# Adding the squares of the latents on VectorE ahead of each latent norm's product with ones

## The chip, the cores and the metric

The kernel runs on one core of a Trainium2 chip. The metric is the device time of one execution in microseconds (us). Before the change the median of three runs is 800.81 us (800.29 to 801.99).

## What is computed

One layer of a decoder trunk on 512 tokens of width 1024: an input projection feeds three branches (a causal pooling mixer, multi-head latent attention, cross-attention into 256 memory tokens), which are gated, merged, projected and added to the residual; then a two-level mixture of experts (32 experts, two per token) and a last RMSNorm. The change touches only the two latent norms of the attention branch, which in the reference are

```
def rms_norm(x, g):
    xf = x.astype(jnp.float32)
    xf = xf * lax.rsqrt(jnp.mean(xf * xf, axis=-1, keepdims=True) + RMS_EPS)
    return xf.astype(x.dtype) * g
...
    c_q = rms_norm(q_down, q_norm_g)
...
    c_kv = rms_norm(kv_down, kv_norm_g)
```

`q_down` has 384 and `kv_down` 256 channels per token, both cut from the input projection of the normalised tokens.

## The kernel before

**Layout.** In the first stage activations stand transposed: a tile has 128 channels on the partitions and the 512 tokens along the free axis. The kv latent is thus two tiles (`zk`), the q latent three (`zq`). The sum of squares over channels is a sum over partitions and tiles. It is made on TensorE (PE) by a product with a 128x128 matrix of ones, which also spreads it to all partitions: one product per tile, accumulated in one PSUM bank.

**Units.** `inproj(c)` (line 278) makes one 128x512 output tile of the input projection. Weights and activations are split into a high and a low fp32r part, so a unit is 24 matmuls of 128x128 by 128x512: 16 on lines 198 and 199 (high weights) and 8 on line 201 (low weights). The weights of unit c+2 are split when unit c is written down: the cast to the high part on ScalarE (ACT, line 180), the subtraction for the low part on GpSimd (POOL, line 125).

**Order of the work.** The whole program stands under a manual schedule: every engine runs its instructions in the order in which the Python code writes them down, and an instruction that waits holds up all that is behind it on its engine. Each unit's result goes to one of four PSUM banks (`mmb`). VectorE (DVE) takes it out by `scaled` (line 283, times the token norm `rx`), then ACT squares it (line 288). Between these stand the preparations of the memory tokens, `mem_prep` (lines 308 to 319): on ACT two scaled copies (line 132) and a square (line 315), on DVE two scalar_tensor_tensor (line 133) and an addition of squares (line 319). `latent_norm` writes the products with ones (line 294), the square root on ACT (line 136) and the reciprocal on DVE (line 137); `latent_end` scales the latent (line 300) and splits it. The places around the two latent norms:

```
    p4 = inproj(4)
    mem_prep(1)
    zq.append(scaled(p3, gt))
    sq_.append(squared(zq[1]))
    rk = latent_norm(sk)
    p5 = inproj(5)
    zq.append(scaled(p4, gt))
    sq_.append(squared(zq[2]))
    for i in range(2):
        latent_end(zk[i], rk, P_KV + i, ckv)
...
        pu = inproj(6 + gi)
        if gi == 0:
            kr = scaled(p5, gt)
            rq = latent_norm(sq_)
            mem_prep(2)
```

So the order on PE is p4, the norm of the kv latent (two products), p5, the first pooling unit pu0, the norm of the q latent (three products), and the other pooling units. DVE lags behind PE: at the kv norm it still has `mem_prep(1)` and the taking out of p3 ahead of it.

**Later stages.** Gates, cross-attention, latent attention and the output projection run up to some 500 us; then come 16 pairs of experts, whose weights (line 686) go by 512 KB pieces into a ring of 40 places, each loaded once its place is free.

Of the kernel before, what the change touches and what calls it, by code (L numbers as in the profile page):

```python
# [14 lines left out]
OP = mybir.AluOpType  # L15
# [26 lines left out]
def trunk_and_moe(ctx, tc, a, out):  # L42
    nc = tc.nc
    v, s, g, pe = nc.vector, nc.scalar, nc.gpsimd, nc.tensor
# [54 lines left out]
    def gt(dt=F32, shape=(128, 512)):  # L99
        return G1.tile(list(shape), dt, tag="g", name=nm("g"), bufs=36)  # L100

    def mt(dt=F32, shape=(128, 512)):
        return G2.tile(list(shape), dt, tag="m", name=nm("m"), bufs=6)
# [7 lines left out]
    def mmb():  # L111
        return bank(PA, "mm", 4)
# [5 lines left out]
    ones = K[:, C_ONES:C_ONES + 128]  # L118
# [16 lines left out]
    def rsqrt(dst, ms, inv):  # L135
        s.activation(dst, ms, AF.Sqrt, bias=eps[:, 0:1], scale=inv)
        v.reciprocal(dst, dst)
# [152 lines left out]

    def latent_norm(sq):
        ps = mmb()
        for i, q in enumerate(sq):
            pe.matmul(ps, lhsT=ones, rhs=q, start=i == 0, stop=i == len(sq) - 1)
        r = gt()
        rsqrt(r, ps, 1.0 / (128 * len(sq)))
        return r
# [41 lines left out]
    ps = mmb()  # L339
# [21 lines left out]
# [5 lines that stand above are left out]
# [11 lines left out]
    for gi, w in enumerate(WINDOWS):  # L377
# [5 lines that stand above are left out]
# [114 lines left out]
    for h_ in range(XHEADS):  # L497
# [3 lines left out]
        ps = mmb()  # L501
# [31 lines left out]
    for h_ in range(XHEADS):  # L533
# [22 lines left out]
        ps = mmb()  # L556
# [78 lines left out]
    for d in range(KD):  # L635
        w = WS.use("w_bpm", d)
        res = []
        for j, y in enumerate((yp, ym)):
            ps = mmb()
# [160 lines left out]
    for h_ in range(HEADS):  # L800
        for op in SEQ:
            k, i = op[0], op[1:]
# [138 lines left out]
    for d in range(KD):  # L941
# [14 lines left out]
        sq = mt()  # L956
# [522 lines left out]
```

## Time and profile before

| | |
|---|---|
| median of 3 runs | 800.81 us (800.29 to 801.99) |
| the profiled execution | 801.2 us, of which the span of the trace is 799.4 us |
| PE busy | 775.8 us, 97% of the span |
| DVE busy | 366.3 us, 46% |
| ACT busy | 303.6 us, 38% |
| POOL busy | 277.1 us, 35% |
| mean granted TensorE clock | 0.992 |

Busy time of an engine says only that it had work in flight. The matmuls are pipelined, so a single matmul's duration is longer than its distance to the next one, and the cost of one is read from the distance of starts. Times in the rows count from the start of the span. "PEld" is the loading of the stationary operand, "PEclk" the granted clock as a share of full speed.

### The profile page before, as it was taken

How to read it: one execution, taken by the hardware profiler on the slowest of the kernel's cores; microseconds unless marked ns; L12 is line 12 of the kernel's file. 1: busy time of each engine (PE TensorE's matmuls, PEld its weight loads, DVE VectorE, ACT ScalarE, POOL GpSimd, SP SyncE). 2: the span in 40 equal slices, each digit the busy share in tenths (PEclk: the TensorE clock that was granted, in tenths of full speed). 3: DMA queues.
4: the chain of work that ended last, by engine and by line, in shares of the span. 5: the costliest groups of instructions: out<-in, count | busy, mean ns of one | idle time of the engine just before them, and what ended most of it. 6: DMA issues, size and time to landing. Idle time of an engine off the chain costs nothing. (4 is left out here: it accounts for less than half of the span.)

```text
span 799.4 us, 10154 instructions
## 1 busy us (share of the span) xinstructions
PE 775.8 (97%) x3743; PEld 523.8 (66%) x3743; DVE 366.3 (46%) x673; ACT 303.6 (38%) x623; POOL 277.1 (35%) x169
## 2 busy tenths in 40 slices
PE   7999999999999999999999999999999999999995
PEld 3778888888887888788888888854333333333432
DVE  5669684243446134677774433142212122454544
ACT  6254354343345544655653321122232223122223
POOL 3156676543241689522222924230212122000000
PEclk8999999999999999999999999999999999999998
DMA  6532333322221322211115379988999999999963
GB/s 220 186 106 106 106 106 132 132 80 80 80 79 43 110 89 82 64 47 57 54 54 211 132 277 342 374 289 307 392 378 383 402 367 388 408 372 390 409 264 121
DMA packets 53509, 164.17 MB, mean 205 GB/s; under 512 B 7906, under 2 KB 9058, under 8 KB 53456
## 3 DMA queue, kind: packets, MB, share of 16 engines
q1 hardware_dynamic: 46224, 149.14, 50.8%
q0 software_dynamic: 4640, 9.90, 3.9%
q10 hardware_dynamic: 2592, 4.46, 1.5%
q8 instruction: 30, 0.49, 0.3%
q14 instruction: 23, 0.19, 0.1%
HBM read 158.82 MB, written 11.53 MB: 213 GB/s over the span
## 5 line engine op out<-in xcount | busy, mean ns | idle before, releaser
L125 POOL TENSOR_TENSOR wl<-r,wh 128x1024 fp32r<-128x1024 f32 (+3 forms) x75 | 167.9, 2245 | 211.2 <-ACT wh L180 191.3
L180 ACT CAST wh<-r 128x1024 fp32r<-128x1024 f32 (+3 forms) x85 | 82.1, 972 | 31.8 <-PE mm L199 12.6
L1131 PE MATMUL gu<-e,u 128*64 128x512 f32 x336 | 88.5, 607 | 1.4 <-DMA e<-in_w_e 1.4
L198 PE MATMUL mm<-g,wh 128*128 128x512 f32 x180 | 71.9, 400 | 0.0
L199 PE MATMUL mm<-g,wh 128*128 128x512 f32 x180 | 70.2, 390 | 0.0
L1107 ACT ACTIVATE u<-xe,PR 128x128 f32<-128x128 f32 x120 | 34.3, 368 | 67.1 <-PE xe L1103 67.0
L471 PE MATMUL mm<-box,wh 128*128 128x512 f32 x144 | 56.8, 394 | 0.9 <-ACT wh L180 0.9
L472 PE MATMUL mm<-box,wh 128*128 128x512 f32 x144 | 56.2, 391 | 0.0
L201 PE MATMUL mm<-g,wl 128*128 128x512 f32 x180 | 52.6, 391 | 0.0
L1161 POOL DMA_INDIRECT xo<-y,ix x9 | 14.3, 1594 | 89.8 <-DVE ix L1082 79.7
L435 ACT ACTIVATE m<-s,st 128x256 f32<-128x256 f32 (+3 forms) x48 | 24.4, 509 | 54.5 <-DVE st L433 54.0
L1131 PEld LDWEIGHTS gu<-e,u 128*64 128x64 f32 x336 | 20.5, 135 | 33.7 <-issue 26.3
L1170 PE MATMUL y<-e,u 128*64 128x512 f32 x160 | 38.6, 600 | 0.6 <-DMA e<-in_w_e 0.6
L201 PEld LDWEIGHTS mm<-g,wl 128*128 128x128 f32 x180 | 33.8, 188 | 7.4 <-POOL wl L125 0.2
L198 PEld LDWEIGHTS mm<-g,wh 128*128 128x128 f32 x180 | 34.0, 189 | 6.4
L199 PEld LDWEIGHTS mm<-g,wh 128*128 128x128 f32 x180 | 33.9, 188 | 6.4
L476 PE MATMUL mm<-box,wl 128*128 128x512 f32 x144 | 36.6, 390 | 0.0
L198 PE MATMUL mm<-box,wh 128*128 128x512 f32 x78 | 31.7, 406 | 0.9 <-DVE g L283 0.9
L1157 DVE TENSOR_SCALAR y<-y,it 128x512 f32<-128x512 f32 x9 | 6.8, 751 | 54.1 <-PE y L1170 54.1
L471 PEld LDWEIGHTS mm<-box,wh 128*128 128x128 f32 x144 | 27.1, 188 | 6.7 <-ACT wh L180 1.3
L476 PEld LDWEIGHTS mm<-box,wl 128*128 128x128 f32 x144 | 27.0, 188 | 5.8
L472 PEld LDWEIGHTS mm<-box,wh 128*128 128x128 f32 x144 | 27.1, 188 | 5.3
(358 smaller groups left out, 1650.2 us busy)
## 6 DMA issues: line engine op xcount, KB each, us to landing
e<-in_w_e SPq DMA_DIRECT2D x124, 512.0 KB
r<-in_w_in SPq DMA_DIRECT2D x37, 512.0 KB
r<-in_w_e SPq DMA_DIRECT2D x15, 512.0 KB
wh<-in_w_e SPq DMA_DIRECT2D x15, 512.0 KB
wl<-in_w_e SPq DMA_DIRECT2D x15, 512.0 KB
m<-in_w_e SPq DMA_DIRECT2D x30, 256.0 KB
r<-in_w_bpm SPq DMA_DIRECT2D x8, 512.0 KB
r<-in_w_bl SPq DMA_DIRECT2D x8, 512.0 KB
```

What stands on the lines that cost most here:

```text
L125: eng.tensor_tensor(lo, x, hi.bitcast(F32), op=OP.subtract)
L180: s.copy(hi[:, :cols], r[:, :cols])
L198: pe.matmul(ps, lhsT=lh, rhs=rh, start=start and i == 0, stop=False)
L199: pe.matmul(ps, lhsT=lh, rhs=rl, start=False, stop=False)
L201: pe.matmul(ps, lhsT=ll, rhs=rh, start=False, stop=stop and i == m - 1)
L435: s.activation(P[:, :w], S[:, :w], AF.Exp, bias=st4[:, 0:1], accum_out=st4[:, 1:2])
L471: pe.matmul(ps, lhsT=lh, rhs=rh, start=k == 0, stop=False)
L472: pe.matmul(ps, lhsT=lh, rhs=rl, start=False, stop=False)
L476: pe.matmul(ps, lhsT=ll, rhs=rh, start=False, stop=k == KD - 1)
L1107: s.activation(x[:, j], ps[:, j], AF.Copy, scale=PR[:, k:k + 1])
L1131: pe.matmul(gu[r], lhsT=self.xe[k // 4][:, k % 4, r], rhs=self.wts[b][k], start=k == 0, stop=k == KD - 1)
L1170: pe.matmul(y[r], lhsT=self.aT[:, k, r], rhs=self.wts[b][8 + 2 * k + hf], start=k == 0 and not more, stop=k == 1)
```

## The change

`latent_norm` adds the squares into the first one on DVE and issues one product with ones. For the kv norm this is one addition and one product where there were two products; for the q norm two additions and one product where there were three.

```
@@ -290,8 +290,9 @@
     def latent_norm(sq):
         ps = mmb()
-        for i, q in enumerate(sq):
-            pe.matmul(ps, lhsT=ones, rhs=q, start=i == 0, stop=i == len(sq) - 1)
+        for q in sq[1:]:
+            v.tensor_tensor(sq[0], sq[0], q, op=OP.add)
+        pe.matmul(ps, lhsT=ones, rhs=sq[0], start=True, stop=True)
         r = gt()
         rsqrt(r, ps, 1.0 / (128 * len(sq)))
         return r
```

The lines below it move down by one: line 294 is now the addition, line 295 the product.

**PE at the kv norm.** In the names, mm_386 is p4, mm_424 the norm's bank, mm_436 p5; g_333 and g_335 are the squares of the kv latent, K holds the ones. Before:

```order
L201 MATMUL mm_386<-u_134,wl_299 128x512
L294 MATMUL mm_424<-g_333,K 128x512 [waits DVE_49,Activation_49]
L294 MATMUL mm_424<-g_335,K 128x512 [waits Activation_49]
L198 MATMUL mm_436<-box_126,wh_337 128x512 [waits DVE_49,Activation_49]
L199 MATMUL mm_436<-box_126,wh_337 128x512
```

and now:

```order
L201 MATMUL mm_386<-u_134,wl_299 128x512
L295 MATMUL mm_424<-g_333,K 128x512 [waits DVE_49]
L198 MATMUL mm_436<-box_126,wh_337 128x512 [waits Activation_49]
L199 MATMUL mm_436<-box_126,wh_337 128x512
L198 MATMUL mm_436<-box_127,wh_337 128x512
```

One product is gone, and the one that stays now reads what DVE wrote last in this place; its wait for ACT's square has become a wait for DVE's addition.

**DVE at the two norms.** g_374 and g_417 belong to `mem_prep(1)`; g_420 is p3 taken out, g_461 p4, g_512 p5; g_427 and g_518 are the two norms; g_378, g_422 and g_463 the squares of the q latent. Before:

```order
L133 SCALAR_TENSOR_TENSOR u_412<-g_192,PR,u_411 128x256 [waits Activation_49] x2
L319 TENSOR_TENSOR g_374<-g_374,g_417 128x512 [waits Activation_49]
L283 TENSOR_TENSOR g_420<-mm_343,g_190 128x512 [waits PE_49]
L137 RECIPROCAL g_427<-g_427 128x512 [waits Activation_49]
L283 TENSOR_TENSOR g_461<-mm_386,g_190 128x512 [waits PE_49]
L300 SCALAR_TENSOR_TENSOR g_329<-g_329,PR,g_427 128x512 [waits DVE_49]
L300 SCALAR_TENSOR_TENSOR g_331<-g_331,PR,g_427 128x512
L283 TENSOR_TENSOR g_512<-mm_436,g_190 128x512 [waits PE_49]
L137 RECIPROCAL g_518<-g_518 128x512 [waits Activation_49]
```

and now:

```order
L133 SCALAR_TENSOR_TENSOR u_412<-g_192,PR,u_411 128x256 [waits Activation_49] x2
L320 TENSOR_TENSOR g_374<-g_374,g_417 128x512 [waits Activation_49]
L283 TENSOR_TENSOR g_420<-mm_343,g_190 128x512 [waits PE_49]
L294 TENSOR_TENSOR g_333<-g_333,g_335 128x512
L137 RECIPROCAL g_427<-g_427 128x512 [waits Activation_49]
L283 TENSOR_TENSOR g_461<-mm_386,g_190 128x512 [waits PE_49]
L301 SCALAR_TENSOR_TENSOR g_329<-g_329,PR,g_427 128x512 [waits DVE_49]
L301 SCALAR_TENSOR_TENSOR g_331<-g_331,PR,g_427 128x512
L283 TENSOR_TENSOR g_512<-mm_436,g_190 128x512 [waits PE_49]
L294 TENSOR_TENSOR g_378<-g_378,g_422 128x512
L294 TENSOR_TENSOR g_378<-g_378,g_463 128x512 [waits DVE_49,Activation_49]
L137 RECIPROCAL g_518<-g_518 128x512 [waits Activation_49]
```

The addition for the kv norm stands behind `mem_prep(1)` and the taking out of p3, those for the q norm behind the taking out of p5.

## Rows read from the trace of the kernel before

**Rows 1.** The page: span, then busy time and share of each engine
```profile
span 799.4 us, 10154 instructions
PE 775.8 (97%) x3743; PEld 523.8 (66%) x3743; DVE 366.3 (46%) x673; ACT 303.6 (38%) x623; POOL 277.1 (35%) x169
```

**Rows 2.** Stages: length, busy of PE, PEld, DVE, ACT, POOL; clock; DMA share; GB/s
```profile
40.00:60.00 20.00, 20.00 (x81) 14.84 (x79) 13.04 (x12) 11.00 (x18) 10.57 (x6) 1.00 0.31 106
80.00:200.00 120.00, 120.00 (x593) 101.41 (x593) 59.68 (x85) 49.28 (x88) 69.19 (x32) 1.00 0.31 106
600.00:700.00 100.00, 96.88 (x437) 34.20 (x437) 23.99 (x67) 26.78 (x78) 18.62 (x17) 1.00 1.02 390
```

**Rows 3.** Whom PE waited for from 62 to 500 us, all of it
```profile
PE mm L471 <- ACT wh L180: 0.9, 1, 0.9
PE tp L761 <- DVE pt L125: 0.8, 1, 0.8
PE tp L761 <- DVE m L439: 0.6, 1, 0.6
PE mm L771 <- ACT pt L129: 0.2, 1, 0.2
```

**Rows 4.** Timeline of PE around the kv norm: start, us, what
```profile
39.22 0.47 PE L198 MATMUL mm<-box,wh 128*128 128x512 f32 x1 [0.92 <-DVE g L283]
...
44.33 0.62 PE L201 MATMUL mm<-u,wl 128*128 128x512 f32 x2
44.79 1.88 PE L294 MATMUL mm<-g,K 128*128 128x512 f32 x4
46.10 0.80 PE L198 MATMUL mm<-box,wh 128*128 128x512 f32 x1
46.74 0.40 PE L199 MATMUL mm<-box,wh 128*128 128x512 f32 x1
46.97 0.40 PE L198 MATMUL mm<-box,wh 128*128 128x512 f32 x1
```

**Rows 5.** Timeline of PE from the end of p5 to behind the q norm
```profile
51.54 0.62 PE L201 MATMUL mm<-u,wl 128*128 128x512 f32 x2
...
56.98 0.62 PE L201 MATMUL mm<-u,wl 128*128 128x512 f32 x2
57.44 2.74 PE L294 MATMUL mm<-g,K 128*128 128x512 f32 x6
59.61 0.79 PE L198 MATMUL mm<-box,wh 128*128 128x512 f32 x1
60.25 0.40 PE L199 MATMUL mm<-box,wh 128*128 128x512 f32 x1
```

**Rows 6.** Timeline of DVE from 38 us to the q norm
```profile
38.39 1.28 DVE L283 TENSOR_TENSOR g<-mm,g 128x512 f32<-128x512 f32 x2
47.08 2.71 DVE L133 SCALAR_TENSOR_TENSOR u<-g,PR,u 128x256 fp32r<-128x256 f32 x2 [2.05 <-ACT u L132]
49.71 0.68 DVE L319 TENSOR_TENSOR g<-g,g 128x512 f32<-128x512 f32 x1
50.31 0.68 DVE L283 TENSOR_TENSOR g<-mm,g 128x512 f32<-128x512 f32 x1
52.27 3.35 DVE L137 RECIPROCAL g<-g 128x512 f32<-128x512 f32 x1 [1.28 <-ACT g L136]
57.40 0.68 DVE L283 TENSOR_TENSOR g<-mm,g 128x512 f32<-128x512 f32 x1
```

**Rows 7.** Timeline of ACT ahead of and behind the kv norm's square root
```profile
46.54 0.91 ACT L132 ACTIVATE u<-g,PR 128x256 fp32r<-128x256 f32 x2
51.56 0.67 ACT L136 ACTIVATE g<-mm,eps 128x512 f32<-128x512 f32 x1
```

**Rows 8.** Timeline of PE at the start, around its first long wait
```profile
1.20 3.59 PE L232 MATMUL mm<-g 128*128 128x512 bf16 x8 [1.20 <-DVE g L227]
9.10 0.80 PE L328 MATMUL mm<-box,wh 128*128 128x512 f32 x1 [4.30 <-ACT box L132]
```

**Rows 9.** Short stretches in which the granted clock changed (columns as in rows 2)
```profile
8.30:8.40 0.10, 0.00 (x0) 0.00 (x0) 0.00 (x0) 0.10 (x2) 0.00 (x0) 0.73 0.99 369
8.60:15.10 6.50, 6.00 (x13) 2.97 (x14) 6.30 (x6) 6.38 (x12) 5.50 (x4) 0.50 0.84 307
15.10:15.20 0.10, 0.10 (x1) 0.03 (x1) 0.10 (x1) 0.10 (x1) 0.00 (x0) 0.64 0.10 41
15.10:793.00 777.90, 766.19 (x3723) 519.81 (x3722) 359.63 (x667) 295.07 (x609) 269.23 (x158) 1.00 0.56 206
```

**Rows 10.** Whom the DMA queue of SyncE waited for, its longest in total
```profile
SPq L167 <- POOL wl L125: 391.3, 75, 16.7
SPq L686 <- DMA e<-in_w_e: 103.8, 91, 2.9
```

More of the change, by code (lines that the diff above doesn't have):

```diff
@@ L292, in latent_norm @@
         ps = mmb()
-        for i, q in enumerate(sq):
-            pe.matmul(ps, lhsT=ones, rhs=q, start=i == 0, stop=i == len(sq) - 1)
+        for q in sq[1:]:
+            v.tensor_tensor(sq[0], sq[0], q, op=OP.add)
+        pe.matmul(ps, lhsT=ones, rhs=sq[0], start=True, stop=True)
         r = gt()
```

## The prediction

> **What bounds the kernel now.** I read the page first: PE is busy 97% of the span, DVE 46% [rows 1]. A busy share says little of a place, so the stages come next: from 40 to 200 us PE has no idle time at all, while the transfers take about 0.3 of the DMA engines; from 600 us on the transfers take all of them, and PE still idles only 3.1 of 100 us [rows 2]. Third the waits of PE: between 62 and 500 us they are four, 2.5 us together [rows 3]. So in the stage of the change the chain that ends last is PE's own queue. What shortens that queue shortens the kernel, what holds it up lengthens it, and 2.5 us at most is there to swallow a hold-up before 500 us.
>
> Then the place itself, on PE, DVE and ACT with one clock. At the kv norm PE runs ahead of DVE: p4's last matmuls start at 44.33 and are done at 44.33 + 0.62 = 44.95, and the norm's products start at 44.79 without a pause [rows 4]. DVE is then still in `mem_prep(1)`: its two products run from 47.08, the addition of line 319 from 49.71, and p3 is taken out from 50.31 [rows 6]. The products with ones could go that early because they needed nothing from DVE's queue but squares made long before.
>
> **What is removed.** The four passes at the kv norm begin at 44.79; p5's second matmul begins at 46.74, the next 0.23 later, so p5's first had its turn at 46.51 [rows 4]. That is 1.72 us for four, 0.43 a pass; a product is two passes, 0.86 us. At the q norm six passes take from 57.44 to 60.25 - 0.23 = 60.02, 2.58 us, 0.43 each again [rows 5]. Removed are one product and two: **-0.86 and -1.72, together -2.58 us**, all on PE's queue.
>
> **What is added at the kv norm.** One addition of 128x512. Line 319 does the same operation on the same size: 0.68 us, and the next DVE instruction starts 0.60 after it [rows 6]. It stands behind the taking out of p3, so it runs from 50.31 + 0.60 = 50.91 to 51.59. A matmul that waited for DVE before began at 39.22, when the first of two results, begun at 38.39, was done at 39.07: 0.15 later [rows 4, 6]. The product with ones thus starts at 51.74 instead of 44.79: **+6.95 us**. Nothing of what sets 50.31 comes from PE's later work: `mem_prep(1)` waits for ACT's copies of 46.54 [rows 6, 7], and p3 was finished before p4. PE cannot use the time, since p5 and pu0 stand behind the waiting product. What is late next on the other engines: the square root, at 51.56 before [rows 7], can begin some 0.86 + 0.15 us behind 51.74, at about 52.75, so ACT and DVE are 1.2 us later while PE is over 6 us later. They get slack, no wait.
>
> **What is added at the q norm.** Two additions, 1.2 us in a row, behind the taking out of p5. A unit takes 56.98 - 51.54 = 5.44 us [rows 5]. If p5 starts at 51.74 + 0.86 = 52.60, it ends near 58.04. DVE's own chain (reciprocal 1.2 us later than 52.27, then p4, two scalings, which ended in the taking out of p5 at 57.40 [rows 6]) frees it at about 58.6 for p5, and the additions end near 58.6 + 0.60 + 1.28 = 60.5. PE gets to the q norm only after pu0, at 58.04 + 5.44 = 63.48. So they cost **nothing**, covered by pu0 with 3 us to spare. Without the first hold-up that cover would be gone: by the old times they would end at 57.40 + 0.60 + 1.28 = 59.28, while PE was there at 57.44, 1.84 us too early.
>
> **The clock.** PE would stand still for 51.74 - 44.95 = 6.8 us. After its first 8 matmuls it stood still from 4.79 (1.20 + 3.59) to 9.10; the granted clock went from 2.4 to 1.2 GHz within 8.30 to 8.40, about 3.6 us into the wait, and came back only at about 15.14, 6.0 us after work began again [rows 8, 9]. Between 15.1 and 793 us no wait was long enough to bring it down [rows 9]. A wait of 6.8 us is longer than that one of 4.3, so I expect the clock to be low when the product starts. At half the clock PE does half the work: up to 6.0 us low costs 3.0; nothing is the other bound, if the clock should hold. In that row weight loads filled only 2.97 of 6.5 us and PE was fed piece by piece; p5 runs unbroken, which should not bring the clock back later. I take 5.0 us low, **+2.5**, near the row.
>
> The Trainium skill ("TensorE: Matmul & The Clock Gate", section "HAM oscillation — how this bites in real kernels") says that waits between bursts of matmuls return the array to the low clock, so that each burst pays again; its example loses half of 1.67 us per burst, and by that figure the clock term would be 0.8 and the sum +5.2. The rule speaks against this change, and rows 8 and 9 show the same with the longer stretch of 6.0 us.
>
> **The sum.** -2.58 + 6.95 + 2.5 = +6.9 us. On the profiled execution's 801.2 that is 808.1; that execution lies 0.4 above the median of 800.81, and on the median it gives **807.7 us**, 0.86% more. It stays to the end because all behind it hangs on PE: the stream of weights waits for splits and for places that PE's work frees [rows 10], so the transfers of the last stage begin later by as much, and their pace, full from 600 us on [rows 2], wins nothing back.
>
> **The rivals.**
> *The wait without the clock.* The clock holds, or falls so shortly that it costs under 1 us: -2.58 + 6.95 = +4.4, 805.2 us. For it: from the start to the end of PE's work it fell only once, and the stretch before was not dense. Against: the wait is longer than the one that did it. Chance 0.15.
> *Won back later.* The whole delay is swallowed where transfers set the pace: 800.8. This needs expert weights that arrive by a clock of their own, as if they were waited for at a fixed time. For it: the transfers are full there [rows 2]. Against: SyncE's queue waits for POOL's splits 391 us in total [rows 10] and for the freeing of places, so it moves with PE; and PE's idle time is too small. Half of it won back would give 804. Chance 0.07.
> *Faster.* Both sets of additions are done before PE asks: only the removed products count, 800.81 - 2.58 = 798.2 us. The point from which it decides is at the kv norm: DVE would have to finish the addition by 44.64 instead of 51.59. For it: the squares are there early and DVE is idle 2.05 us before 47.08 [rows 6]. Against: the order is fixed, and the addition stands behind p3. If only the kv norm were free, the q norm would wait 1.84 + 0.15 us, and the sum would be -0.6, no change. Chance 0.05.
>
> **How the numbers follow.** Forecast 0.73, clock held 0.15, won back 0.07, faster 0.05. A measurement here tells about 0.2% (1.6 us) from no change. Won back splits evenly over no change and a little slower; of faster, 0.01 goes to no change. That gives faster 0.04, same 0.04, slower 0.92. The range takes in the held clock at its lower end (805.2, less 0.5 for a reading of starts and for the runs) and at its upper end the full 3.0 of the clock, 808.2, with 1.5 for waits that the shift makes elsewhere: 804.7 to 809.7.
>
> **What would show it.** Right: PE idle about 6.8 us just before line 295 at the kv norm, with DVE's line 294 as the releaser; that addition from about 50.9; a granted clock of half near 52 us and full again by about 57; no wait at line 295 of the q norm; both norms' passes 10 before, 4 now; PE without further new waits, all later stages 6 to 7 us later. Wrong: an addition that runs before p3 is taken out, a clock of 1.0 throughout, or an end of the expert stage that has moved by much less than the end of the q norm.

## The result and the profile after

The changed kernel takes 808.81 us (median of 6 executions, 806.79 to 811.68), the kernel before beside it 800.72 (6 executions, 800.29 to 802.75): a ratio of 1.0096, 95% interval 1.0076 to 1.0117, so 0.96% slower. The forecast was 807.7, the range 804.7 to 809.7.

The page of the changed kernel, first lines:

```profile
span 808.8 us, 10142 instructions
PE 778.3 (96%) x3737; PEld 526.1 (65%) x3737; DVE 367.8 (45%) x676; ACT 303.5 (38%) x623; POOL 278.1 (34%) x169
```

The page names six PE instructions fewer (three products of two passes) and three more on DVE, as written; the span is 9.4 us longer than in [rows 1]. Where, the timeline of PE shows; the first five rows answer to [rows 4], the last two to [rows 5]:

```profile
44.30 0.61 PE L201 MATMUL mm<-u,wl 128*128 128x512 f32 x2
51.56 2.07 PE L295 MATMUL mm<-g,K 128*128 128x512 f32 x2 [6.64 <-DVE g L294]
52.65 1.42 PE L198 MATMUL mm<-box,wh 128*128 128x512 f32 x1
53.86 0.63 PE L199 MATMUL mm<-box,wh 128*128 128x512 f32 x1
54.29 0.63 PE L198 MATMUL mm<-box,wh 128*128 128x512 f32 x1
...
65.45 1.02 PE L295 MATMUL mm<-g,K 128*128 128x512 f32 x2
65.90 0.79 PE L198 MATMUL mm<-box,wh 128*128 128x512 f32 x1
```

p4 ends where it did, then PE stands still 6.64 us, released by DVE's addition. At the q norm it does not wait. DVE, answering to [rows 6]:

```profile
47.06 2.65 DVE L133 SCALAR_TENSOR_TENSOR u<-g,PR,u 128x256 fp32r<-128x256 f32 x2 [2.04 <-ACT u L132]
49.63 0.68 DVE L320 TENSOR_TENSOR g<-g,g 128x512 f32<-128x512 f32 x1
50.23 0.68 DVE L283 TENSOR_TENSOR g<-mm,g 128x512 f32<-128x512 f32 x1
50.83 0.68 DVE L294 TENSOR_TENSOR g<-g,g 128x512 f32<-128x512 f32 x1
...
60.80 0.73 DVE L294 TENSOR_TENSOR g<-g,g 128x512 f32<-128x512 f32 x1
62.06 1.17 DVE L294 TENSOR_TENSOR g<-g,g 128x512 f32<-128x512 f32 x1 [0.52 <-ACT wh L180]
```

The addition starts 0.60 behind the taking out of p3 and is done at 51.51; PE starts 0.05 later. The q norm's additions are done at 63.23, 2.2 us before PE asks at 65.45.

The clock, by stretches of the changed kernel (length; busy of PE, PEld, DVE, ACT, POOL; PEclk; DMA share; GB/s), first at the kv norm, then in the routing stage, in which the tokens are assigned to experts ahead of the expert products:

```profile
46.00:48.00 2.00, 0.00 (x0) 0.00 (x0) 0.94 (x1) 1.94 (x4) 1.31 (x1) 1.00 0.17 70
48.00:50.00 2.00, 0.00 (x0) 0.00 (x0) 2.00 (x3) 0.00 (x0) 1.03 (x1) 0.74 0.00 0
50.00:52.00 2.00, 0.44 (x1) 0.44 (x2) 1.51 (x3) 0.63 (x1) 0.00 (x0) 0.50 0.77 262
52.00:54.00 2.00, 2.00 (x4) 0.87 (x4) 0.00 (x0) 0.33 (x1) 0.00 (x0) 0.50 0.00 0
54.00:56.00 2.00, 2.00 (x7) 1.57 (x6) 1.60 (x1) 1.30 (x2) 0.63 (x1) 0.55 0.00 0
56.00:58.00 2.00, 2.00 (x11) 1.64 (x10) 2.00 (x2) 0.00 (x0) 1.77 (x1) 1.00 0.00 0
...
536.50:537.00 0.50, 0.00 (x1) 0.01 (x1) 0.44 (x4) 0.00 (x0) 0.00 (x0) 1.00 1.12 402
537.00:537.50 0.50, 0.50 (x3) 0.50 (x3) 0.00 (x0) 0.00 (x0) 0.00 (x0) 0.57 0.89 340
...
543.00:543.50 0.50, 0.50 (x4) 0.50 (x3) 0.00 (x0) 0.00 (x0) 0.00 (x0) 0.50 0.15 33
543.50:544.00 0.50, 0.50 (x4) 0.26 (x5) 0.00 (x0) 0.17 (x1) 0.00 (x0) 0.60 0.00 0
```

It was at 1.2 GHz before the product began and until about 55.8, 4.2 us into the work. And it fell once more, from about 537.1 to 543.9, where in the profiled execution of before it held at full [rows 9]. PE's waits from 500 us on are the same in both kernels to 0.2 us. The second row below, 1.2 us for `ix`, is the wait at whose end, at 537.0, the clock fell; the kernel before has the same wait. The other two rows lie among the experts. Of the changed kernel:

```profile
PE gu L1132 <- DMA e<-in_w_e: 1.6, 2, 1.3
PE at L1078 <- DVE ix L1083: 1.2, 1, 1.2
PE y L1171 <- DMA e<-in_w_e: 0.5, 2, 0.4
```

To split the 9.4 us I take two marks. The first mark is the start of p4's last pair of matmuls, 44.33 before [rows 4] and 44.30 after. The second is the first gate matmul, at 77.2 and 83.4 (a line's matmuls: count, shortest, median and longest in ns, first and last start; before, then after):

```profile
L471 PE MATMUL mm<-box,wh x144: 387/389/500, 77.2 to 268.3; 128*128 128x512 f32 x144
```

```profile
L472 PE MATMUL mm<-box,wh x144: 387/389/497, 83.4 to 274.6; 128*128 128x512 f32 x144
```

Between the marks are 77.2 - 44.33 = 32.9 and 83.4 - 44.30 = 39.1 us: **+6.2 us** in the stage of the change. From there to the last gate matmul of the line it is 191 us in both. The other 3.1 us come later, near to half of the 6.8 us at half clock near 540. These are the two profiled executions; the medians differ by 8.1 us, so that in them some 1.9 us lie behind the stage. Below, "stage" is this distance from p4's last pair to the first gate matmul, less 32.9; it leaves out what the start and the later stages of an execution do.

### The profile page after: what moved, and what is told of

Its sections match the earlier page's. It is cut to its first block, busy times and chain, and to the rows that moved or that the text cites. A ratio compares the mean times of both kernels' runs of the same rounds, so it can differ in the third digit from the quotient of the medians.

```text
span 808.8 us, 10142 instructions
## 1 busy us (share of the span) xinstructions
PE 778.3 (96%) x3737; PEld 526.1 (65%) x3737; DVE 367.8 (45%) x676; ACT 303.5 (38%) x623; POOL 278.1 (34%) x169
## 5 line engine op out<-in xcount | busy, mean ns | idle before, releaser
L472 PE MATMUL mm<-box,wh 128*128 128x512 f32 x144 | 56.8, 394 | 0.9 <-ACT wh L180 0.9
L473 PE MATMUL mm<-box,wh 128*128 128x512 f32 x144 | 56.3, 391 | 0.0
L198 PE MATMUL mm<-box,wh 128*128 128x512 f32 x78 | 32.8, 420 | 0.5 <-DVE g L283 0.5
L472 PEld LDWEIGHTS mm<-box,wh 128*128 128x128 f32 x144 | 27.1, 188 | 6.7 <-ACT wh L180 1.3
L199 PE MATMUL mm<-box,wh 128*128 128x512 f32 x78 | 31.0, 397 | 0.0
```

The costliest lines, as they stand in the source:

```text
L198: pe.matmul(ps, lhsT=lh, rhs=rh, start=start and i == 0, stop=False)
L199: pe.matmul(ps, lhsT=lh, rhs=rl, start=False, stop=False)
L472: pe.matmul(ps, lhsT=lh, rhs=rh, start=k == 0, stop=False)
L473: pe.matmul(ps, lhsT=lh, rhs=rl, start=False, stop=False)
```

## The experiments

The question: is it the place of the kv norm's addition in DVE's queue and the clock behind that wait, as forecast, or do DVE's additions cost by themselves; and what are the last 3 us? All kernels ran with executions of the kernel before on the same chip, whose median in the three groups was 801.14, 801.08 and 801.17 us (single executions 798.7 to 805.9). In the table "PE's wait" is the one at the latent norms, unless it says otherwise; the kernels whose names end in rfill have 5 more matmuls in the routing stage. Twelve kernels:

| kernel | median us | ratio to before, 95% interval | PE's wait, us | stage, us |
|---|---|---|---|---|
| kv_only | 809.05 | 1.0095, 1.0065 to 1.0125 | 6.65 | +7.6 |
| q_only | 804.76 | 1.0044, 1.0027 to 1.0060 | 3.50 | +3.4 |
| kv_filled | 804.88 | 1.0042, 1.0022 to 1.0063 | filled, 0.61 left | +4.3 |
| early_kv | 807.31 | 1.0066, 1.0041 to 1.0090 | 4.27 | +3.4 |
| early_two | 800.14 | 0.9980, 0.9967 to 0.9994 | none | -1.4 |
| early_late | 801.12 | 0.9999, 0.9987 to 1.0012 | 0.7, a gate unit | -1.1 |
| after_rfill | 807.34 | 1.0073, 1.0057 to 1.0089 | 6.7 | +6.3 |
| before_rfill | 800.94 | 0.9995, 0.9987 to 1.0004 | none | 0 |
| q_nopool | 801.31 | 1.0001, 0.9986 to 1.0016 | 1.9 | +0.7 |
| two_rfill | 799.75 | 0.9974, 0.9961 to 0.9987 | none | -1.4 |
| late_rfill | 800.49 | 0.9984, 0.9971 to 0.9996 | 0.7, a gate unit | -0.9 |
| filled_rfill | 805.70 | 1.0048, 1.0031 to 1.0065 | filled, 0.6 left | +4.3 |

### One norm at a time: kv_only, q_only

The edit of kv_only against the changed kernel; in q_only the condition is 3:

```
+        if len(sq) == 2:
             for q in sq[1:]:
                 v.tensor_tensor(sq[0], sq[0], q, op=OP.add)
             pe.matmul(ps, lhsT=ones, rhs=sq[0], start=True, stop=True)
+        else:
+            for i, q in enumerate(sq):
+                pe.matmul(ps, lhsT=ones, rhs=q, start=i == 0, stop=i == len(sq) - 1)
```

> The changed kernel, with the addition only at the kv norm; the q norm keeps its three products. My theory (the whole loss is PE's wait at the kv norm and the low clock behind it): PE idles 6.6 us ahead of the kv norm's product and the clock is at half until some 4 us behind it, as in the changed kernel, and the three products at the q norm cost 1.72 us more than there: start of the first pooling unit behind the q norm 8.0 us later than before, 809 to 811 us. Rival (each added DVE addition costs by itself, since DVE is behind): one addition of three, a third of the loss, 803 to 804 us.

> The changed kernel, with the additions only at the q norm; the kv norm keeps its two products. My theory: the additions end near 59.3 us, PE asks at 57.4, so it waits 1.9 to 2.0 us and wins 1.72: +0.3 us, 800.7 to 801.5, and the clock stays at full there, since the wait is short. Rival (cost by the addition): two of three, 805 to 806 us. Rival (the q norm is covered by the pooling unit in itself): no wait, -1.7, 799 us.

kv_only came as expected: the whole loss is there with one addition of three, so it does not go by the count of additions. Its wait:

```profile
PE mm L296 <- DVE g L295: 6.7, 1, 6.7
```

q_only did not come as expected: 804.76 instead of some 801. Its wait, its DVE and POOL, POOL's three subtractions in the kernel before, and its clock:

```profile
PE mm L296 <- DVE g L295: 3.5, 1, 3.5
```

```profile
57.34 0.68 DVE L283 TENSOR_TENSOR g<-mm,g 128x512 f32<-128x512 f32 x1
57.94 3.04 DVE L295 TENSOR_TENSOR g<-g,g 128x512 f32<-128x512 f32 x2
...
57.49 4.62 POOL L125 TENSOR_TENSOR g<-g,g 128x512 fp32r<-128x512 f32 x3 [1.91 <-ACT g L129]
```

```profile
57.56 3.77 POOL L125 TENSOR_TENSOR g<-g,g 128x512 fp32r<-128x512 f32 x3 [1.91 <-ACT g L129]
```

```profile
58.00:60.00 2.00, 0.00 (x0) 0.00 (x0) 1.90 (x3) 1.54 (x3) 2.00 (x2) 1.00 0.05 21
60.00:62.00 2.00, 0.97 (x1) 0.50 (x2) 0.98 (x1) 0.00 (x0) 2.00 (x2) 0.69 0.01 4
62.00:64.00 2.00, 2.00 (x5) 1.24 (x4) 0.13 (x1) 0.85 (x2) 2.00 (x2) 0.50 0.03 8
```

DVE starts the additions when it was expected to, at 57.94, but the two take 3.04 us, 1.52 each, beside three POOL subtractions, which take 4.62 together where they took 3.77 before the change. PE waits 3.5 us, not 1.9, and in this execution the clock falls, at about 60.8, and is full again near 64.2. The product starts at 61.03 instead of 57.44, +3.6; less the 1.72 of the two products, plus half of the 3.1 us of work at half clock, 1.5: +3.4, which is what the stage lost.

### Is it POOL: q_nopool

The three POOL subtractions are issued behind the q norm instead of ahead of it.

```
-        split(h, l, z, g)
+        s.copy(h, z)
+        held.append((l, z, h))
...
             rq = latent_norm(sq_)
+            for e in held:
+                sub_lo(*e, g)
```

> The kernel with the additions at the q norm alone, and three POOL subtractions (low parts of the two kv latents and of the pooling weights, line 125) moved behind the q norm in POOL's queue, so that POOL stands idle while DVE adds. In the kernel without the move the two additions took 1.5 us each beside them, where a lone one takes 0.68, and PE waited 3.5 us. Theory (DVE's additions and POOL's subtractions slow each other): the additions take 0.7 each, PE waits 1.9 to 2.0 us, the clock holds, and the time is +0.3 over before, about 801 us. Rival (the additions are slow there by themselves): still 1.5 each, 3.5 us of wait, 804 to 805 us.

DVE and POOL of this kernel:

```profile
57.91 1.47 DVE L295 TENSOR_TENSOR g<-g,g 128x512 f32<-128x512 f32 x2
...
59.59 2.38 POOL L125 TENSOR_TENSOR wl<-r,wh 128x1024 fp32r<-128x1024 f32 x1 [4.04 <-ACT wh L180]
61.92 3.81 POOL L125 TENSOR_TENSOR g<-g,g 128x512 fp32r<-128x512 f32 x3
```

```profile
PE mm L296 <- DVE g L295: 1.9, 1, 1.9
```

With POOL idle the additions take 1.47 together and PE waits 1.9 us; the clock stays at full from the kv norm on through the whole of the routing stage. The time is that of the kernel before (1.0001), the wait against the two products. That DVE's additions and POOL's subtractions slow each other is thus shown, and with it why q_only lost: 1.6 us more of waiting, and the clock that fell in the longer wait.

### The clock behind the wait: kv_filled

```
+        if len(sq) == 2:
+            for _ in range(28):
+                pe.matmul(ps, lhsT=KB[:, 0:128], rhs=KB, start=True, stop=True)
         pe.matmul(ps, lhsT=ones, rhs=sq[0], start=True, stop=True)
```

> The changed kernel, with 28 bf16 matmuls of 128x128 by 128x512 into the kv norm's own bank ahead of its product, as work for PE while it waits (they are overwritten). 28 by some 0.22 us is 6.2 us, less than the wait of 6.6. My theory: the product starts at the same time, 51.6, but the granted clock stays at full, and the half of the 4.2 us that the changed kernel spends at half clock behind the product comes back: 2.1 us less than the changed kernel, about 805 us where the clock does not fall later on. Rival (the clock cost nothing, the wait and something in the later stages cost all): the same as the changed kernel, 807 to 811.

PE and the clock of this kernel:

```profile
43.69 6.22 PE L297 MATMUL mm<-KB 128*128 128x512 bf16 x28
50.52 1.13 PE L298 MATMUL mm<-g,K 128*128 128x512 f32 x2 [0.61 <-DVE g L294]
```

```profile
50.00:52.00 2.00, 1.48 (x5) 0.92 (x6) 0.47 (x1) 0.85 (x2) 0.00 (x0) 1.00 0.38 154
52.00:54.00 2.00, 2.00 (x10) 1.64 (x9) 1.60 (x1) 1.30 (x2) 0.62 (x1) 1.00 0.00 0
```

The useful work waits as long, but the clock holds, and the stage loses 4.3 instead of 6.2 us. The clock at this place costs 1.9 us, close to half of the 4.2 us of work at half clock.

### The place in the queue: early_kv

```
     sk = [squared(z) for z in zk]
+    v.tensor_tensor(sk[0], sk[0], sk[1], op=OP.add)
...
-    rk = latent_norm(sk)
+    rk = latent_norm(sk[:1], 2)
```

> The changed kernel, with the kv norm's addition written right behind the two squares, ahead of the memory preparation on DVE; the q norm as in the change. My theory (it is the place of the addition in DVE's queue, not the addition): no wait at the kv norm, -0.86 us there; the q norm then waits: PE asks 0.86 us earlier than before, at 56.6, the additions end near 59.3, so it waits 2.8 and wins 1.72: about +0.3 over the kernel before, 800.7 to 801.5, clock at full from 15 us on. Rival (DVE has no room for the addition): later squares and reciprocals on DVE, 802 or more.

PE at the kv norm, then DVE and PE at the q norm (line 383 holds its additions):

```profile
44.59 0.62 PE L201 MATMUL mm<-u,wl 128*128 128x512 f32 x2
45.06 1.02 PE L294 MATMUL mm<-g,K 128*128 128x512 f32 x2
...
58.27 1.37 DVE L383 TENSOR_TENSOR g<-g,g 128x512 f32<-128x512 f32 x1
60.16 1.15 DVE L383 TENSOR_TENSOR g<-g,g 128x512 f32<-128x512 f32 x1 [0.52 <-ACT wh L180]
...
61.37 2.08 PE L294 MATMUL mm<-g,K 128*128 128x512 f32 x2 [4.27 <-DVE g L383]
```

The wait at the kv norm is gone, so it was the place, not the addition. The total is no gain all the same: PE comes to the q norm earlier and meets there what q_only met, additions of 1.37 and 1.15 us beside POOL, a wait of 4.27 us and the clock at half from about 60.9 to 64.3. The stage loses 3.4, as in q_only: where PE waits at the q norm for DVE, it goes on when DVE is done, whatever was saved ahead of it. The median is higher than the stage alone explains; in its profiled execution the clock also fell near 535.4, for some 3.4 us.

### Versions that keep the gain: early_two, early_late

early_two, beside the early kv addition:

```
     sq_.append(squared(zq[1]))
+    v.tensor_tensor(sq_[0], sq_[0], sq_[1], op=OP.add)
...
-            rq = latent_norm(sq_)
+            rq = latent_norm(sq_[::2], 3)
```

> The kv norm's addition right behind its squares; at the q norm the first two squares are added as soon as the second is made, and two products with ones are issued (the added pair, the third square). Nothing that PE asks for then stands late in DVE's queue. My theory: one product less at either norm and no new wait, -1.72 us: 799.0 us, below the kernel before. Rival (PE's queue is not what ends last, the later stages swallow it): 800.7, no difference.

early_late adds all three in the old place and issues the product behind the next unit:

```
-            rq = latent_norm(sq_)
+            for q in sq_[1:]:
+                v.tensor_tensor(sq_[0], sq_[0], q, op=OP.add)
...
         if gi == 1:
+            rq = latent_norm(sq_[:1], 3)
             mem_prep(3)
```

> As the one with the early kv addition, and all three squares of the q latent added as in the change, but the q norm's one product is issued behind the second pooling unit, one unit of 5.4 us later, when the additions are long done. My theory: all three products are saved and none is waited for, -2.58 us: 798.2 us. Rival: the q norm's root and reciprocal come 5 us later on ACT and DVE, and PE waits for them or for what they push back: 799 to 801.

early_two is faster than the kernel before, 0.9980, by 1.4 us in the stage where 1.72 were expected; in the median it is 0.9 us. early_late is not, though it saves a product more. Its trace has a new wait:

```profile
PE mm L474 <- DVE m L408: 0.7, 1, 0.7
```

The q norm's reciprocal of 3.3 us now runs on DVE at 68.06 between two results of pooling units, so DVE is later at the first gate unit and PE waits 0.7 us for a bank. That is half of the 1.5 us that are missing in the stage. The place of the reciprocal as the cause of this wait is read from the order on DVE and not tested; where the rest went is open.

### The last 3 us: after_rfill, before_rfill and the other kernels with it

```
             elif op[0] == "b":
+                if n_ == 2:
+                    fill_ps = bank(PC, "cb", 1)
+                    for _ in range(5):
+                        pe.matmul(fill_ps, lhsT=KB[:, 0:128], rhs=KB, start=True, stop=True)
```

> The changed kernel, with 5 bf16 matmuls into a bank that nobody reads, at the point of the routing stage (some 536 us) where PE waits 1.2 us for DVE and where the clock of the changed kernel's profiled execution fell to half for 6.4 us. My theory (executions of the changed kernel near 810 us are those in which the clock falls there, those near 806 the ones in which it holds, and the wait itself is the same as before the change): it falls less often, the executions gather at 805 to 807, median about 806. Rival (the spread has another cause, in the transfers): still 806.8 to 811.7 with a median near 808.8.

> The same 5 matmuls in the kernel before. My theory: the clock held there in the profiled execution of the kernel before, so nothing to win: 800.3 to 801, at most the few executions near 802 go. Rival (the matmuls cost time at that place): 801.5 or more, which would have to be taken off the reading of the changed kernel with them.

> The version with one product less at either norm and nothing late in DVE's queue, with the 5 matmuls in the routing stage. Theory: -1.4 to -1.7 us by the products, and the executions in which the clock falls in the routing stage are gone: 799.3 us, below both kernels clear of their spread. Rival: no better than the version without the 5 matmuls, 800.1.

> The version that issues the q norm's one product a unit later, with the 5 matmuls in the routing stage. That version won nothing in the median (801.1), though its profiled execution came out 1.6 us shorter than that of before. Theory (a new wait of PE for DVE of 0.7 us at the first gate unit gives part back, and clock falls in the routing stage hide the rest): 799.5 to 800. Rival (the later root and reciprocal cost it all): 801.

> The changed kernel with both fillings, 28 matmuls in PE's wait at the kv norm and 5 in the routing stage: the wait is there, the clock is at full in both places. Theory: what is left is the wait less the removed products, 6.6 + 0.2 - 2.6 = +4.2 us over the kernel before with the same 5 matmuls (800.9): 805, and executions within 2 us of each other. Rival (a cause of its own in the expert stage): over 806.5.

In these kernels the 5 matmuls stand where PE otherwise waits 1.2 us for `ix`. With them none of the five profiled executions shows the clock falling in the routing stage; without them it fell in three of nine, those of the changed kernel, q_only and early_kv. In all three it had fallen at a norm as well; kv_only is the one of the nine in which it fell at a norm alone, and in the other five it fell at neither.

What such a fall costs can be read right behind it. From the last matmul of line 889 (lines as numbered before) to the first `at<-INF,P` of line 1077 it is 30.8 us in the kernel before and 30.9 in kv_only and kv_filled; in the changed kernel, with 6.8 us at half clock, it is 34.0, and in q_only and early_kv, with 3.4 us, 32.5. The 3.1 us of the changed kernel are thus the clock. Further on other differences come in: to the last expert product it is 279.9 to 280.6 us where the clock fell and 276.7 to 278.9 where it held, and the 278.9 is two_rfill, without a fall.

In the medians the effect is not settled. after_rfill came out at 807.34 (806.32 to 808.94), neither the 806 of the expectation nor the 808.8 of its rival; it lies below the changed kernel's 808.81, but was not run beside it. It is 6.4 us above before_rfill, which ran in its group, and 6.3 is what its stage loses. For the kernel before the 5 matmuls change nothing (0.9995), only its executions reach from 800.0 to 801.9 instead of 800.2 to 804.6. filled_rfill, with the clock at full in both places of its profile, ends at 805.70, +4.3 in its stage, as the wait less the removed products gives; it is no faster than kv_filled without the 5 matmuls (1.0048 against 1.0042). two_rfill has the lowest ratio of all, 0.9974 with an interval of 0.9961 to 0.9987 (799.75 us, where 799.3 was expected).

## Why the prediction was right

**The sign and the size** came from one step: the addition stands behind `mem_prep(1)` and p3 in DVE's queue while PE is already there. Forecast: addition at 50.91, PE idle 6.8 us, product 6.95 us later. Measured: 50.83, 6.64 and 51.56 - 44.79 = 6.8. The hand-over took 0.05 us, not the 0.15 that I took from the matmul that had waited before [rows 4, 6].

**The removed products**: four passes now instead of ten, and at the q norm the next unit's second high-weight matmul (60.48 before, 66.77 after) is 6.3 us later; with 6.8 from the wait and 1.9 from the clock (kv_filled) the sum of the steps is 6.8 + 1.9 - 2.58 = 6.1. The gain of 2.58 fits what was computed, and it was paid for three times over.

**The clock at the kv norm**: forecast +2.5 (5.0 us at half), measured 1.9 (4.2 us at half). The rival in which it holds fell with the row at 50 us. The ground for it was weaker than it looked: a wait of 4.3 us at the start [rows 8] was taken to bring the clock down, and in half of the profiled executions a wait of that length there did not (last section).

**The q norm**: forecast no wait, and there is none; the spare time is 2.2 us, not 3. One step behind it was wrong: "Without the first hold-up that cover would be gone: by the old times they would end at 57.40 + 0.60 + 1.28 = 59.28". q_only shows them ending at 57.94 + 3.04 = 60.98. The step took an addition's price from a row where POOL was idle, line 319 at 49.71; beside POOL's subtractions it is 1.5 us. In the changed kernel that place is hidden behind the first wait, so the sum did not notice. The "faster" rival's side branch (-0.6 if only the kv norm were free) falls with it: early_kv is that case, and it loses 3.4 in the stage.

**"PE without further new waits"** held. The 3.1 us beyond the stage are the clock in the routing stage, which I had not costed: I read 1.00 over 15 to 793 us in one execution [rows 9] as a property of the kernel. The profile with the fall is of an execution of 810.53 us; others end near 806.8, but of those there is no profile, so that they are clear of the fall is likely and not shown. The median of 808.81 is 1.1 above the forecast, and the expert stage won nothing back. That the median is so near is in part luck: the stage cost 6.2 us where 6.9 were forecast, some 1.9 us came from behind it, where the forecast had nothing, and the upper end of the range had 1.5 us for waits elsewhere, of which there were none. Whether the change makes that fall more frequent is open: the executions of before also reach up to 805.9, and one profile per kernel is too few to count, though all three falls came in executions whose clock had fallen at a norm.

## What to carry to other kernels

Before a sum is moved from the engine that sets the end to an idler one, look at where the idler engine's queue stands when the result is asked for, not at how busy it is: DVE was 46% busy and 6 us behind. Put the added instruction where its inputs are ready and the queue is waiting anyway, as early_two does, and price it beside whatever runs on POOL at that moment. A wait of PE also has to be priced with the clock behind it, as a range, since equal waits ended with the clock up and down. A clock that held in one profile can fall in the next.

## What the runs showed of the hardware

- DVE's addition of 128x512 took 0.68 us alone and 1.52 us beside POOL's fp32 subtractions of the same size; POOL slowed too, from 3.77 to 4.62 us for three. The Trainium skill ("SBUF — State Buffer", section "SBUF: two separate sides") says that a DVE instruction with two SBUF inputs and a POOL instruction that reads SBUF exclude each other for the whole instruction. The trace of q_only fits that: the 4.62 us in which both ran are near to, and 0.35 short of, 3.77 + 2 x 0.60 = 4.97 one after the other, and q_nopool, where POOL was idle, has the short additions. Beside POOL's subtractions of 128x1024, 2.4 us each alone, one such addition took 2.89 us (early_late, at 64.65). The prediction had not drawn on it.
- At the norms PE waits of 3.5, 4.27 and 6.6 to 6.7 us ended with the granted clock at 1.2 GHz; one of 1.9 us, in q_nopool, did not. But the length of a wait did not decide it: at the start of the kernel every profiled execution has a wait of 3.7 to 4.8 us, and in seven of fourteen the clock held at 2.4 GHz. The changed kernel, then q_only, each with that wait and the clock behind it:

```profile
PE mm L329 <- ACT box L132: 4.8, 1, 4.8
10.00:12.00 2.00, 2.00 (x6) 0.93 (x5) 2.00 (x2) 2.00 (x6) 2.00 (x3) 0.50 0.94 316
...
PE mm L333 <- ACT box L132: 4.8, 1, 4.8
10.00:12.00 2.00, 2.00 (x6) 0.94 (x5) 2.00 (x2) 2.00 (x6) 2.00 (x3) 1.00 0.95 302
```

- At the norms PE worked some 3 to 4.2 us before it had the clock back; at the start of the kernel before it was 6.0 us.
- The clock also fell behind a wait of only 1.2 us (537.0, after short matmuls of the routing stage); in the profiled execution of before, with the same wait, it held.
